# The first stage of a decoder trunk: x loaded and turned by quarters of its channels instead of by halves

## The chip, the core and the metric

The kernel runs on one core of one Trainium2 chip. The core has TensorE (PE, with its weight loads on the separate row PEld), VectorE (DVE), ScalarE (ACT), GpSimd (POOL) and SyncE (SP). SP and ACT each issue transfers on a queue of their own, and all transfers run on the same 16 DMA engines. The metric is the device time of one execution in microseconds (us). In the trace, times are counted from the start of the span.

## The reference, cut to what matters

One decoder layer is computed for a prompt of 512 positions and for 8 samples of 8 positions, 576 rows of 1024 channels in all, with the same weights. In float32:

```python
mod = silu(c) @ w_ada + b_ada               # c: 1 prompt row and 8 sample rows
sh1, sc1, g1, sh2, sc2, g2 = split(mod, 6)
u = x * (1 + sc1) + sh1                     # shared input of both token mixers
z = u @ w_in                                # [pool | q | f | i | out_gate | gate_A | gate_B]
y_pool = pool_mixer(z_pool)                 # 512 channels, causal means over 2, 4, 8, 16 tokens
y_hgrn = hgrn2(z_q, z_f, z_i, z_og, lb)     # lb from softmax(lb_logits)
x = layer_norm(ALPHA * x + g1 * (merged @ w_out))
x = layer_norm(ALPHA * x + g2 * (silu(h @ w_gate) * (h @ w_up)) @ w_down)   # h = x * (1 + sc2) + sh2
```

The change lies wholly in the first stage: from the loads of x, c and the small vectors to z_pool, the first 512 columns of z.

## The kernel before, in words

**Channels on partitions.** u is wanted with its 1024 channels on the partitions, as 8 blocks of 128 channels (kt = 0 to 7) by 576 columns. x comes with its rows on partitions, in tiles of 128 rows by 512 channels (four of the prompt, one of 64 rows of the samples); `x_load` loads one half of the channels (5 tiles), and `x_turn` turns a half on TensorE into PSUM (L304, L309) and copies it to XT on ACT and DVE (L305, L311).

**Scale and shift.** `ada` makes 256 columns of mod: w_ada comes in two tiles of 512 KB, eight products with c go side by side on the array (L339), the four partial rows are copied out (adaev, L343) and summed by another product (L345), and the bias is added (mod, L347). A pair of channel blocks needs one such block of sc1 and one of sh1. ACT then makes uh, the part of u that is rounded for the fast product (L397), and u itself (L402); DVE makes the sample columns (L398 to L401) and ul, the remainder u - uh (L403).

**Products.** Each weight tile is split in the same way: whi on ACT (L111), wlo on DVE (L112). A product is three matmuls: wlo by uh, whi by ul, whi by uh. For z_pool the five row tiles of u are the stationary operand and 512 columns of w_in the moving one; the sums of all 8 channel blocks stay in five PSUM banks (zp, L417). The loop over b = 0 to 3 handles two channel blocks each: it makes u for the pair, runs `ada1(b + 1)` for the next pair, then the pair's 30 products. I call the four pairs quarter 0 to quarter 3. After quarter 3 the weights of z_f follow (L154), and then the rest of the layer.

**What sets the order.** The tile layer schedules the recorded instructions with a timeline of its own, so the order on an engine is not that of the code. Every engine runs its instructions in order. A tile with a number of buffers is reused in turn: the weight tiles raw, whi and wlo have 3 buffers, the w_ada tiles 8, the x tiles 10, and the PSUM tile t, in which x is turned and `ada` sums, has 2. The transfers of SP and ACT take turns on eight completion semaphores; each transfer waits until the one eight places before it has landed.

**Queues.** Before the change SP issues c, the first half of x, w_ada for quarter 0 (with six small vectors, `rows`, between its two blocks: b_ada, lb_logits, norm weights and the like, L285), the first tile of w_in, w_ada for quarter 1, the second half of x, the second tile of w_in, and so on. ACT issues the constants (cst, L98) and a copy of the old pooling state.

Of the kernel before, what the change touches and what calls it, by code (L numbers as in the profile page):

```python
# [12 lines left out]
P = 128  # L13
D = 1024
KT = D // P
TP = 512
# [57 lines left out]
def trunk(tc, consts, x_prompt, x_sample, state_pool, state_hgrn, c_prompt, c_sample,  # L74
# [20 lines left out]
    sp.dma_start(out=cc[0:1], in_=c_prompt)  # L95
    sp.dma_start(out=cc[1:9], in_=c_sample)
    cst = t_(cp, [P, C_END], "cst")
    act.dma_start(out=cst, in_=consts[:, 0:C_END])  # L98
    ident = cst[:, C_ID:C_ID + P]
    rows = t_(s0, [92, P], "rows")  # L100
    R_LB, R_NW, R_PS, R_BA, R_LG, R_LO, R_END = 0, 16, 24, 28, 76, 84, 92
    cst_eps = t_(cp, [P, 2], "eps")
# [159 lines left out]
    def x_load(j):  # L262

        xin = []
        for i in range(5):
            n = P if i < 4 else TS
            xt = t_(sx, [P, 512], "x", bufs=10)
            c = slice(j * 512, (j + 1) * 512)
            sp.dma_start(out=xt[:n], in_=x_prompt[0, i * P:(i + 1) * P, c] if i < 4 else xs_flat[:, c])
            xin.append(xt)  # L270
        return xin

    ada_ready = {}

    def ada_pre(b):
        for m in (SC1, SH1):
            ada_ready[m // 2 + b] = ada_load(s0, m // 2 + b)
        return ada_last[0]

    xin = [x_load(0)]  # L280
    ada_ready[SC1 // 2] = ada_load(s0, SC1 // 2)
    for r, src in ((R_BA, b_ada[0]), (R_LB, lb_logits.rearrange("r c -> (r c)")), (R_NW, hgrn_norm_w[0]),
                   (R_PS, pool_scale[0]), (R_LG, ln1_g[0]), (R_LO, ln1_b[0])):
        v = src.rearrange("(h p) -> h p", p=P)
        sp.dma_start(out=rows[r:r + v.shape[0]], in_=v)  # L285
    ada_ready[SH1 // 2] = ada_load(s0, SH1 // 2)
    w0 = [load_w(seq.pop(0))]
    ada_pre(1)
    xin.append(x_load(1))
    w0.append(load_w(seq.pop(0)))  # L290
    ada_pre(2)
    w0.append(load_w(seq.pop(0)))
    late = ada_pre(3)
# [6 lines left out]
    def x_turn(q):  # L300
        for i in range(4):
            ps = t_(psA, [P, 512], "t", bufs=2)
            for k in range(4):
                pe.transpose(out=ps[:, k * P:(k + 1) * P], in_=xin[q][i][:, k * P:(k + 1) * P], identity=ident)  # L304
            (dve.tensor_copy if i % 2 else act.copy)(out=XT[:, 4 * q:4 * q + 4, i * P:(i + 1) * P],  # L305
                                                     in_=ps.rearrange("p (k n) -> p k n", k=4))
        ps = t_(psA, [P, 512], "t", bufs=2)
        for k in range(4):
            pe.transpose(out=ps[:, k * TS:(k + 1) * TS], in_=xin[q][4][:TS, k * P:(k + 1) * P],  # L309
                         identity=ident[:TS, :TS])  # L310
        act.copy(out=XT[:, 4 * q:4 * q + 4, TP:T], in_=ps[:, :4 * TS].rearrange("p (k n) -> p k n", k=4))  # L311

    x_turn(0)
# [11 lines left out]

    mod = t_(cp, [P, 48, 9], "mod")
# [39 lines left out]

    lbt = t_(cp, [P, 6, 8], "lbt")
    lmax, le0, le1, lb, oml, noml = (lbt[:, i] for i in range(6))
    dve.tensor_tensor(out=lmax, in0=prow[:, 0:8], in1=prow[:, 8:16], op=ALU.max)
    dve.tensor_tensor(out=le0, in0=prow[:, 0:8], in1=lmax, op=ALU.subtract)  # L370
    dve.tensor_tensor(out=le1, in0=prow[:, 8:16], in1=lmax, op=ALU.subtract)
    act.activation(out=lbt[:, 1:3], in_=lbt[:, 1:3], func=AF.Exp)
    dve.tensor_tensor(out=lmax, in0=le0, in1=le1, op=ALU.add)
    dve.reciprocal(out=oml, in_=lmax)
    dve.tensor_tensor(out=lb, in0=le0, in1=oml, op=ALU.mult)
    dve.tensor_tensor(out=oml, in0=le1, in1=oml, op=ALU.mult)
    dve.tensor_scalar(out=noml, in0=oml, scalar1=-1.0, scalar2=None, op0=ALU.mult)

# [10 lines left out]
    for b in range(4):  # L389
        us_ = []  # L390
        for kt in (2 * b, 2 * b + 1):
# [11 lines left out]
            dve.tensor_tensor(out=UL[:, kt], in0=u, in1=UH[:, kt].bitcast(F32), op=ALU.subtract)  # L403
        if b < 3:
            ada1(b + 1)
        if b == 0:
# [899 lines left out]
```

## Time and profile before

| | us |
|---|---|
| median of 3 runs | 1022.06 |
| the runs | 1018.23, 1022.06, 3328.05 |
| the profiled execution | 1022.08 |
| its span | 1020.2 |
| TensorE busy | 972.8 (95%) |
| VectorE busy | 784.0 (77%) |
| ScalarE busy | 489.5 (48%) |

A busy share is an average over the span. The first stage lasts until the first product of z_f starts at 63.88 us; what is said of it is read from the chain of waits, the timeline and the DMA rates of that stretch.

### The profile page before, as it was taken

How to read it: one execution, taken by the hardware profiler on the slowest of the kernel's cores; microseconds unless marked ns; L12 is line 12 of the kernel's file. 1: busy time of each engine (PE TensorE's matmuls, PEld its weight loads, DVE VectorE, ACT ScalarE, POOL GpSimd, SP SyncE). 2: the span in 40 equal slices, each digit the busy share in tenths (PEclk: the TensorE clock that was granted, in tenths of full speed). 3: DMA queues.
4: the chain of work that ended last, by engine and by line, in shares of the span. 5: the costliest groups of instructions: out<-in, count | busy, mean ns of one | idle time of the engine just before them, and what ended most of it. 6: DMA issues, size and time to landing. Idle time of an engine off the chain costs nothing.

```text
span 1020.2 us, 17282 instructions
## 1 busy us (share of the span) xinstructions
PE 972.8 (95%) x6675; PEld 887.6 (87%) x6675; DVE 784.0 (77%) x1337; ACT 489.5 (48%) x889; POOL 355.4 (35%) x263
## 2 busy tenths in 40 slices
PE   6999999999999999998988988999999999999995
PEld 3689899999999998778987778999999999788884
DVE  3662989988998664349797788999999998946548
ACT  3454675577656763334333354544444445533330
POOL 0012777677676855724671102222222220000000
PEclk9999999999999999999999999999999999999998
DMA  8951243323332359952318400233233323432202
GB/s 272 313 143 33 69 114 113 87 83 112 101 107 86 103 168 307 293 175 75 92 52 271 131 1 21 83 105 103 84 91 98 103 84 111 139 120 68 90 32 93
DMA packets 157748, 120.54 MB, mean 118 GB/s; under 512 B 3885, under 2 KB 136585, under 8 KB 157659
## 3 DMA queue, kind: packets, MB, share of 16 engines
q1 hardware_dynamic: 155695, 114.67, 37.3%
q10 hardware_dynamic: 1972, 4.78, 1.4%
q8 instruction: 52, 0.85, 0.3%
q14 instruction: 29, 0.24, 0.1%
HBM read 111.15 MB, written 8.40 MB: 117 GB/s over the span
## 4 chain that ended last, share of the span: by engine, by line
PE 63%; DVE 18%; DMA 6%; ACT 5%; issue 5%; POOL 2%; SPq 0%; DVEq 0%; POOLq 0%; ACTq 0%
PE b L217 24%; PE f L217 10%; PE b L1164 4%; PE b L1163 4%; PE b L1162 4%; DMA ada<-in_w_ada 3%; PE z L154 3%; PE zp L417 3%; ACT whi L172 2%; DVE wlo L173 2%; DVE tmp L560 2%; DVE S L658 1%; PE s L723 1%; DVE qz L587 1%; PE b L1168 1%
## 5 line engine op out<-in xcount | busy, mean ns | idle before, releaser
L172 ACT CAST whi<-st 128x512 fp32r<-128x512 f32 x184 | 108.8, 616 | 57.5 <-PE b L217 13.3
L173 DVE TENSOR_TENSOR wlo<-st,whi 128x512 fp32r<-128x512 f32 x140 | 113.4, 835 | 9.7 <-ACT whi L172 4.4
L217 PE MATMUL f<-uh,whi 128*128 128x288 f32 x352 | 105.9, 301 | 0.0
L217 PE MATMUL f<-ul,whi 128*128 128x288 f32 x352 | 104.9, 298 | 0.0
L217 PE MATMUL f<-uh,wlo 128*128 128x288 f32 x352 | 104.1, 296 | 0.0
L197 POOL TENSOR_TENSOR st<-raw 128x512 f32<-128x512 f32 x36 | 55.0, 1528 | 137.7 <-DVE wlo L173 60.8
L172 ACT CAST whi<-raw 128x1024 fp32r<-128x1024 f32 x46 | 48.3, 1050 | 98.1 <-PE b L217 55.5
L112 DVE TENSOR_TENSOR wlo<-raw,whi 128x1024 fp32r<-128x1024 f32 (+1 forms) x49 | 57.9, 1182 | 29.1 <-ACT whi L111 28.0
L198 POOL TENSOR_TENSOR st<-st,raw 128x512 f32<-128x512 f32 x46 | 64.2, 1396 | 39.7 <-issue 37.7
L111 ACT CAST whi<-raw 128x1024 fp32r<-128x1024 f32 (+1 forms) x49 | 48.0, 979 | 58.0 <-PE z L154 9.8
L1164 PE MATMUL b<-whi,hl 128*128 128x512 f32 (+1 forms) x198 | 72.6, 367 | 0.0
L1163 PE MATMUL b<-whi,hl 128*128 128x512 f32 (+1 forms) x198 | 72.5, 366 | 0.0
L1162 PE MATMUL b<-wlo,hl 128*128 128x512 f32 (+1 forms) x198 | 72.4, 365 | 0.0
L203 POOL TENSOR_TENSOR st<-raw,st 128x512 f32<-128x512 f32 x26 | 42.4, 1632 | 85.9 <-DVE wlo L173 85.9
L173 DVE TENSOR_TENSOR wlo<-raw,whi 128x1024 fp32r<-128x1024 f32 x46 | 57.3, 1246 | 18.9 <-ACT whi L172 18.7
L217 PEld LDWEIGHTS f<-uh,whi 128*128 128x128 f32 x352 | 66.1, 188 | 4.5 <-issue 1.7
L217 PEld LDWEIGHTS f<-ul,whi 128*128 128x128 f32 x352 | 66.1, 188 | 3.5 <-issue 3.4
L217 PEld LDWEIGHTS f<-uh,wlo 128*128 128x128 f32 x352 | 66.1, 188 | 2.8 <-issue 2.5
L173 POOL TENSOR_TENSOR wlo<-st,whi 128x512 fp32r<-128x512 f32 x44 | 58.3, 1333 | 5.7 <-ACT whi L172 5.2
L217 PE MATMUL b<-bh,whi 128*128 128x288 f32 x184 | 55.1, 300 | 2.1 <-ACT bh L172 2.1
L217 PE MATMUL b<-bl,whi 128*128 128x288 f32 x184 | 54.3, 296 | 0.0
L217 PE MATMUL b<-bh,wlo 128*128 128x288 f32 x184 | 54.1, 295 | 0.0
(454 smaller groups left out, 3180.8 us busy)
## 6 DMA issues: line engine op xcount, KB each, us to landing
raw<-in_w_in SPq DMA_DIRECT2D x52, 512.0 KB
ada<-in_w_ada SPq DMA_DIRECT2D x16, 1024.0 KB
raw<-in_w_gate SPq DMA_DIRECT2D x22, 512.0 KB
raw<-in_w_down SPq DMA_DIRECT2D x22, 512.0 KB
ada<-in_w_ada SPq DMA_DIRECT2D x16, 512.0 KB
raw<-in_w_up SPq DMA_DIRECT2D x12, 512.0 KB
rawu<-in_w_up SPq DMA_DIRECT2D x10, 512.0 KB
s<-in_state_hgrn SPq DMA_DIRECT2D x8, 512.0 KB
```

The lines of the kernel that those rows point to most:

```text
L111: act.copy(out=hi[:, :n], in_=raw[:, :n])
L112: eng.tensor_tensor(out=lo[:, :n], in0=raw[:, :n], in1=hi[:, :n].bitcast(F32), op=ALU.subtract)
L154: mm = pe.matmul(out=ps[:, GA0 + c0:GA0 + c1], lhsT=a[:, kt * P:(kt + 1) * P], rhs=x[:, kt, c0:c1], start=first and i == 0, stop=last and ...
L172: act.copy(out=hi, in_=src)
L173: return eng.tensor_tensor(out=lo, in0=src, in1=hi.bitcast(F32), op=ALU.subtract)
L197: pool.tensor_tensor(out=s1, in0=a21, in1=a22, op=ALU.add)
L198: pool.tensor_tensor(out=s2, in0=s1, in1=a11, op=ALU.subtract)
L203: eng.tensor_tensor(out=s4, in0=a12, in1=s2, op=ALU.subtract)
L217: pe.matmul(out=ps, lhsT=x[:, k * P:(k + 1) * P], rhs=y[:, k], start=first and k + i == 0, stop=last and k == 3 and i == 2)
L1162: pe.matmul(out=o, lhsT=xh, rhs=lo, start=first, stop=False)
L1163: pe.matmul(out=o, lhsT=xl, rhs=hi, start=False, stop=False)
L1164: return pe.matmul(out=o, lhsT=xh, rhs=hi, start=False, stop=last)
```

## The change

x comes in four quarters of 256 channels (five tiles of 128 rows by 256 channels each, still ten buffers). `quarter_load` issues for one quarter: x, the two blocks of w_ada, the tile of w_in. Two quarters are issued ahead, the others from inside the loop. c and the six small vectors are issued by ACT, ahead of its first table load. `x_turn(0)` stands behind the turning of c. The lower bound (lbt) is written behind the loop.

```diff
--- before.py
+++ after.py
@@ -92,13 +92,17 @@
     s0, _s0 = pl.open("s0", "right")
     sx, _sx = pl.open("sx", "right")
     cc = t_(s0, [9, D], "cc")
-    sp.dma_start(out=cc[0:1], in_=c_prompt)
-    sp.dma_start(out=cc[1:9], in_=c_sample)
     cst = t_(cp, [P, C_END], "cst")
     act.dma_start(out=cst, in_=consts[:, 0:C_END])
+    act.dma_start(out=cc[0:1], in_=c_prompt)
+    act.dma_start(out=cc[1:9], in_=c_sample)
     ident = cst[:, C_ID:C_ID + P]
     rows = t_(s0, [92, P], "rows")
     R_LB, R_NW, R_PS, R_BA, R_LG, R_LO, R_END = 0, 16, 24, 28, 76, 84, 92
+    for r, src in ((R_BA, b_ada[0]), (R_LB, lb_logits.rearrange("r c -> (r c)")), (R_NW, hgrn_norm_w[0]),
+                   (R_PS, pool_scale[0]), (R_LG, ln1_g[0]), (R_LO, ln1_b[0])):
+        v = src.rearrange("(h p) -> h p", p=P)
+        act.dma_start(out=rows[r:r + v.shape[0]], in_=v)
     cst_eps = t_(cp, [P, 2], "eps")
     dve.memset(cst_eps[:, 0:1], RMS_EPS)
     dve.memset(cst_eps[:, 1:2], LN_EPS)
@@ -264,33 +268,24 @@
         xin = []
         for i in range(5):
             n = P if i < 4 else TS
-            xt = t_(sx, [P, 512], "x", bufs=10)
-            c = slice(j * 512, (j + 1) * 512)
+            xt = t_(sx, [P, 256], "x", bufs=10)
+            c = slice(j * 256, (j + 1) * 256)
             sp.dma_start(out=xt[:n], in_=x_prompt[0, i * P:(i + 1) * P, c] if i < 4 else xs_flat[:, c])
             xin.append(xt)
         return xin
 
-    ada_ready = {}
-
-    def ada_pre(b):
+
+    xin, ada_ready, w0 = [], {}, []
+
+    def quarter_load(b):
+        xin.append(x_load(b))
         for m in (SC1, SH1):
             ada_ready[m // 2 + b] = ada_load(s0, m // 2 + b)
+        w0.append(load_w(seq.pop(0)))
         return ada_last[0]
 
-    xin = [x_load(0)]
-    ada_ready[SC1 // 2] = ada_load(s0, SC1 // 2)
-    for r, src in ((R_BA, b_ada[0]), (R_LB, lb_logits.rearrange("r c -> (r c)")), (R_NW, hgrn_norm_w[0]),
-                   (R_PS, pool_scale[0]), (R_LG, ln1_g[0]), (R_LO, ln1_b[0])):
-        v = src.rearrange("(h p) -> h p", p=P)
-        sp.dma_start(out=rows[r:r + v.shape[0]], in_=v)
-    ada_ready[SH1 // 2] = ada_load(s0, SH1 // 2)
-    w0 = [load_w(seq.pop(0))]
-    ada_pre(1)
-    xin.append(x_load(1))
-    w0.append(load_w(seq.pop(0)))
-    ada_pre(2)
-    w0.append(load_w(seq.pop(0)))
-    late = ada_pre(3)
+    quarter_load(0)
+    quarter_load(1)
 
     psA, _psA = pl.open("psA", space=PSUM)
 
@@ -298,19 +293,20 @@
     XT = t_(s0, [P, KT, T], "xt")
 
     def x_turn(q):
-        for i in range(4):
+        for i in (0, 2):
             ps = t_(psA, [P, 512], "t", bufs=2)
-            for k in range(4):
-                pe.transpose(out=ps[:, k * P:(k + 1) * P], in_=xin[q][i][:, k * P:(k + 1) * P], identity=ident)
-            (dve.tensor_copy if i % 2 else act.copy)(out=XT[:, 4 * q:4 * q + 4, i * P:(i + 1) * P],
-                                                     in_=ps.rearrange("p (k n) -> p k n", k=4))
+            for j in range(2):
+                for k in range(2):
+                    pe.transpose(out=ps[:, k * 256 + j * P:k * 256 + (j + 1) * P],
+                                 in_=xin[q][i + j][:, k * P:(k + 1) * P], identity=ident)
+            (dve.tensor_copy if i else act.copy)(out=XT[:, 2 * q:2 * q + 2, i * P:(i + 2) * P],
+                                                 in_=ps.rearrange("p (k n) -> p k n", k=2))
         ps = t_(psA, [P, 512], "t", bufs=2)
-        for k in range(4):
+        for k in range(2):
             pe.transpose(out=ps[:, k * TS:(k + 1) * TS], in_=xin[q][4][:TS, k * P:(k + 1) * P],
                          identity=ident[:TS, :TS])
-        act.copy(out=XT[:, 4 * q:4 * q + 4, TP:T], in_=ps[:, :4 * TS].rearrange("p (k n) -> p k n", k=4))
-
-    x_turn(0)
+        act.copy(out=XT[:, 2 * q:2 * q + 2, TP:T], in_=ps[:, :2 * TS].rearrange("p (k n) -> p k n", k=2))
+
 
     sc_ = t_(s0, [9, D], "sc")
     act.activation(out=sc_, in_=cc, func=AF.Sigmoid)
@@ -323,6 +319,7 @@
     dve.tensor_copy(out=cpad[:, :, 0:9],
                     in_=pc[:, :P].rearrange("p (k c) -> p k c", c=16)[:, :, 0:9])
 
+    x_turn(0)
     mod = t_(cp, [P, 48, 9], "mod")
 
     dr, _dr = pl.open("gada", space=bass.MemoryType.DRAM)
@@ -363,19 +360,6 @@
 
     ps0 = [t_(psA, [P, 512], "zp", bufs=5) for i in range(5)]
     ada1(0)
-
-    lbt = t_(cp, [P, 6, 8], "lbt")
-    lmax, le0, le1, lb, oml, noml = (lbt[:, i] for i in range(6))
-    dve.tensor_tensor(out=lmax, in0=prow[:, 0:8], in1=prow[:, 8:16], op=ALU.max)
-    dve.tensor_tensor(out=le0, in0=prow[:, 0:8], in1=lmax, op=ALU.subtract)
-    dve.tensor_tensor(out=le1, in0=prow[:, 8:16], in1=lmax, op=ALU.subtract)
-    act.activation(out=lbt[:, 1:3], in_=lbt[:, 1:3], func=AF.Exp)
-    dve.tensor_tensor(out=lmax, in0=le0, in1=le1, op=ALU.add)
-    dve.reciprocal(out=oml, in_=lmax)
-    dve.tensor_tensor(out=lb, in0=le0, in1=oml, op=ALU.mult)
-    dve.tensor_tensor(out=oml, in0=le1, in1=oml, op=ALU.mult)
-    dve.tensor_scalar(out=noml, in0=oml, scalar1=-1.0, scalar2=None, op0=ALU.mult)
-
     YA = t_(ym, [P, 4, T], "ya")
     YB = t_(ym, [P, NH, T], "yb")
 
@@ -401,11 +385,14 @@
             dve.tensor_copy(out=UH[:, kt, TP:T], in_=u[:, TP:T])
             act.activation(out=u[:, 0:TP], in_=XT[:, kt, 0:TP], func=AF.Identity, scale=sc[:, 0:1], bias=sh[:, 0:1])
             dve.tensor_tensor(out=UL[:, kt], in0=u, in1=UH[:, kt].bitcast(F32), op=ALU.subtract)
+        if b < 2:
+            late = quarter_load(b + 2)
         if b < 3:
+            x_turn(b + 1)
             ada1(b + 1)
+        if b == 2:
+            pl.close(_sx)
         if b == 0:
-            x_turn(1)
-            pl.close(_sx)
             tu, _tu = pl.open("tu", "left")
             TU = t_tiles(tu, ("t1", "t2", "t4"))
         for kt in (2 * b, 2 * b + 1):
@@ -425,9 +412,19 @@
                 dve.tensor_tensor(out=tc_[:, k], in0=u[:, HT:T], in1=tc_[:, k], op=ALU.subtract)
         for n, t, k0, k1 in ((), (("t1", ta, 0, 4),), (("t2", tb, 0, 2),), ())[b]:
             split(*(x[:, k0:k1] for x in TU[n]), t[:, k0:k1])
-        if b == 0:
-            w0.append(load_w(seq.pop(0)))
     pl.close(_s0)
+
+    lbt = t_(cp, [P, 6, 8], "lbt")
+    lmax, le0, le1, lb, oml, noml = (lbt[:, i] for i in range(6))
+    dve.tensor_tensor(out=lmax, in0=prow[:, 0:8], in1=prow[:, 8:16], op=ALU.max)
+    dve.tensor_tensor(out=le0, in0=prow[:, 0:8], in1=lmax, op=ALU.subtract)
+    dve.tensor_tensor(out=le1, in0=prow[:, 8:16], in1=lmax, op=ALU.subtract)
+    act.activation(out=lbt[:, 1:3], in_=lbt[:, 1:3], func=AF.Exp)
+    dve.tensor_tensor(out=lmax, in0=le0, in1=le1, op=ALU.add)
+    dve.reciprocal(out=oml, in_=lmax)
+    dve.tensor_tensor(out=lb, in0=le0, in1=oml, op=ALU.mult)
+    dve.tensor_tensor(out=oml, in0=le1, in1=oml, op=ALU.mult)
+    dve.tensor_scalar(out=noml, in0=oml, scalar1=-1.0, scalar2=None, op0=ALU.mult)
 
     def zt():
         return t_(psZ, [P, D], "z", bufs=2)
```

On all five engines the instructions from the first product of z_f on stand in the same order as before; what moves lies ahead of it. Three places.

ACT, between the u of quarter 0 and that of quarter 1 (whi is the rounded weight tile, raw the loaded one, uh the rounded u, xt the turned x). Before:

```order
L402 ACTIVATE yb_266<-xt_165,mod_211 128x512
L111 CAST whi_136<-raw_134 128x1024
L305 COPY xt_165<-t_307 128x4x128
L397 ACTIVATE uh_84<-xt_165,mod_211 128x512
L402 ACTIVATE yb_266<-xt_165,mod_211 128x512
L397 ACTIVATE uh_84<-xt_165,mod_211 128x512
```

Now:

```order
L386 ACTIVATE yb_220<-xt_143,mod_175 128x512
L302 COPY xt_143<-t_257 128x2x256
L115 CAST whi_136<-raw_134 128x1024
L308 COPY xt_143<-t_269 128x2x64
L115 CAST whi_253<-raw_251 128x1024
L115 CAST whi_374<-raw_372 128x1024
L381 ACTIVATE uh_90<-xt_143,mod_175 128x512
```

The casts of the third and fourth weight tiles (raw_251, raw_372) now stand ahead of quarter 1's uh; before, they stood behind it. On DVE the remainder of the fourth tile now stands ahead of quarter 1's ul:

```order
L116 TENSOR_TENSOR wlo_375<-raw_372,whi_374 128x1024
L385 CAST uh_90<-yb_220 128x64 x2
L302 COPY xt_143<-t_384 128x2x256
L407 TENSOR_TENSOR yb_220<-yb_220 128x288
L387 TENSOR_TENSOR ul_91<-yb_220,uh_90 128x576 x2
```

ACT, ahead of quarter 0, now (t is the PSUM tile with two buffers, in which x_turn and `ada` take turns):

```order
L302 COPY xt_143<-t_159 128x2x256
L115 CAST whi_112<-raw_110 128x1024
L308 COPY xt_143<-t_171 128x2x64
L422 ACT_TABLE_LOAD
L422 ACTIVATE lbt_604<-lbt_604 128x16
L381 ACTIVATE uh_90<-xt_143,mod_175 128x512
```

The copy of the turned sample tile out of t_171 stands behind the cast of the first weight tile, and the first product of `ada` (t_191) takes t_171's buffer. The exponential of the lower bound still stands ahead of quarter 0's u.

SP, the third round of loads, now:

```order
L273 DMA x_241<-in_x_sample 64x256
L261 DMA ada_243<-in_w_ada 128x4x256
L261 DMA ada_245<-in_w_ada 128x4x256
L129 DMA raw_251<-in_w_in 128x2x512
L261 DMA ada_247<-in_w_ada 128x4x256
L129 DMA raw_372<-in_w_in 128x2x512
L261 DMA ada_249<-in_w_ada 128x4x256
```

The fourth weight tile, raw_372, is loaded behind three quarters of x, eleven tiles of w_ada and three of w_in.

## Rows read from the trace of the kernel before

**Rows 1.** Chain of waits, 0 to 110 us: start us, us, what

```profile
23.82 2.43 PE zp L417 x5
...
37.03 0.44 PE t L304 x4
37.47 3.66 PE zp L417 x16
41.13 0.39 PE t L309 x4
41.52 1.00 PE t L339 x16
...
63.88 6.39 PE z L154 x48
```

**Rows 2.** Timeline, ACT's first casts, one product: start, us, engine, operation, [idle before, releaser]

```profile
18.07 1.08 PE L339 MATMUL t<-ada,cpad 128*32 128x256 f32 x8 [0.53 <-DMA ada<-in_w_ada]
...
19.70 1.04 ACT L111 CAST whi<-raw 128x1024 fp32r<-128x1024 f32 x1 [3.72 <-DMA raw<-in_w_in]
...
30.83 1.05 ACT L111 CAST whi<-raw 128x1024 fp32r<-128x1024 f32 x1 [5.71 <-DMA raw<-in_w_in]
```

**Rows 3.** DMA issues by line, 0 to 80 us: tile, source, count, KB each

```profile
ada<-in_w_ada SPq DMA_DIRECT2D x16, 512.0 KB
raw<-in_w_in SPq DMA_DIRECT2D x11, 512.0 KB
x<-in_x_prompt SPq DMA_DIRECT2D x8, 256.0 KB
...
cst<-in_consts ACTq DMA_DIRECT2D x1, 263.0 KB
```

**Rows 4.** DMA totals of three windows: 0 to 18, 0 to 31, 0 to 36 us

```profile
DMA packets 3357, 4.23 MB, mean 235 GB/s; under 512 B 244, under 2 KB 2416, under 8 KB 3349
...
DMA packets 7029, 8.71 MB, mean 281 GB/s; under 512 B 425, under 2 KB 5219, under 8 KB 7020
...
DMA packets 8655, 10.47 MB, mean 291 GB/s; under 512 B 475, under 2 KB 6698, under 8 KB 8646
```

**Rows 5.** Busy time by stretch; the last three columns: granted clock, DMA share, GB/s

```profile
12.00:13.00 1.00, 0.91 (x8) 0.81 (x8) 0.00 (x0) 0.98 (x2) 0.00 (x0) 1.00 0.39 86
...
30.00:36.00 6.00, 5.81 (x37) 4.66 (x34) 2.86 (x8) 2.56 (x4) 0.00 (x0) 1.00 1.09 353
```

**Rows 6.** Timeline, SP's queue: first of the six small vectors, next w_ada tile

```profile
7.00 0.33 SPq L285 DMA_DIRECT2D rows<-in_b_ada  x1
...
11.64 1.93 SPq L257 DMA_DIRECT2D ada<-in_w_ada  x2
```

**Rows 7.** Groups by shape, 0 to 64 us: busy us, mean ns of one, idle before

```profile
L112 DVE TENSOR_TENSOR wlo<-raw,whi 128x1024 fp32r<-128x1024 f32 x6 | 7.3, 1220 | 1.5 <-ACT whi L111 1.3
...
L397 ACT ACTIVATE uh<-xt,mod 128x512 fp32r<-128x512 f32 x8 | 6.5, 807 | 9.9 <-DVE mod L347 9.9
...
L403 DVE TENSOR_TENSOR ul<-yb,uh 128x576 fp32r<-128x576 f32 x4 | 3.0, 751 | 0.4 <-ACT yb L402 0.4
L305 DVE COPY xt<-t 128x512 f32<-128x512 f32 x4 | 2.8, 689 | 4.1 <-PE t L304 4.1
...
L420 DVE TENSOR_TENSOR yb<-yb 128x288 f32<-128x288 f32 x4 | 1.8, 450 | 0.0
...
L401 DVE CAST uh<-yb 128x64 fp32r<-128x64 f32 x4 | 0.6, 188 | 0.0
```

**Rows 8.** Timeline, TensorE after two idle times: start, us, operation, [idle before]

```profile
524.70 0.58 PE L217 MATMUL f<-t3h,whi 128*128 128x288 f32 x1 [2.05 <-DVE u L230]
...
539.61 0.38 PE L217 MATMUL f<-t3h,whi 128*128 128x288 f32 x1 [1.98 <-DVE u L230]
```

**Rows 9.** Busy time by stretch, behind each of those two

```profile
524.70:528.00 3.30, 3.30 (x14) 3.30 (x15) 3.30 (x4) 1.77 (x3) 2.22 (x2) 0.50 0.11 40
...
536.00:543.00 7.00, 5.02 (x38) 4.82 (x37) 6.76 (x12) 4.29 (x5) 0.24 (x1) 1.00 0.46 165
```

## The prediction

> **What bounds the kernel now.** I read the chain of waits first. In the first stage it runs from the first product at 23.82 us almost without a break along TensorE to 63.88 us, where z_f starts [rows 1]; ahead of 23.82 it runs along transfers. The timeline gives the two places where ACT sat before a weight cast and waited for the transfer: 3.72 us until 19.70 for the first tile, 5.71 us until 30.83 for the second [rows 2]. The list of DMA issues gives the sizes [rows 3], the DMA totals how much had moved by then [rows 4], and the busy time by stretch the rates, 86 GB/s at 12 to 13 us and 353 GB/s later [rows 5]. So the stage is transfers up to 23.8 us, then TensorE, fed by transfers with some us to spare. The instructions behind 63.88 us stand in the old order, so I take a shift of that point as the shift of the end. The profiled execution took 1022.08 us, the median is 1022.06, so either may be the base.
>
> **When a tile lands.** Count KB in the order of issue. Up to the first weight tile stood half of x (four tiles of 256 KB and one of 128), four w_ada tiles, the weights themselves, the constants [rows 3], and about 194 KB of small transfers: 4169 KB, 4.27 MB. It was there at 19.70, when the DMA had moved 4.23 MB by 18 us [rows 4] and 1.7 us at 353 GB/s [rows 5] more, 4.83 in all. The second tile: 7881 KB, 8.07 MB, there at 30.83, with 8.71 MB moved by 31 us, so 8.65 at that time. In both cases a tile was there when 0.56 to 0.58 MB more had moved than stood up to it. I use 0.58.
>
> **The change part by part.**
>
> *Smaller head.* Up to the first weight tile now stand 576 KB less of x: 3593 KB, 3.68 MB, so 4.26 MB must have moved. On the old curve that is 18.1 us.
>
> *Small vectors to ACT's queue.* SP had w_ada waiting behind six small transfers, from 7.00 to 11.64 us [rows 6], and the DMA fell to 86 GB/s for the microsecond from 12 [rows 5]. At 353 GB/s that gap is 0.8 us; I take it as gained, with bounds of 0 (the gap stays) and 1.5 us (some of the slow stretch around it goes as well). The first tile is then there at 17.3 instead of 19.7 us. [...]
>
> *ACT's longer start.* Eight issues at about SP's 0.33 us each [rows 6], some with a wait, stand ahead of the table load and the sigmoid of c. That puts c's turning at 10 to 11 us. Products with c need the first w_ada tiles anyway, and, see next, something later: cost nothing; without this cover 2 us.
>
> *Quarter 0.* The first product of `ada` takes the PSUM buffer of the turned sample tile, whose copy stands on ACT behind the first weight cast. So it starts at 17.3 + 1.05 + about 0.5 = 18.9 us instead of before the weights. Before, from a group of eight such products at 18.07 [rows 2] to the first z product took 5.75 us; now the other block's 16 records come on top, 2.2 us at 1.08 per eight. First z product at 26.8 us, later than the old 23.82, at most; it is 2 to 3 us earlier if TensorE is at its full clock by then, at which 16 such records take 1.00 us [rows 1]. Quarter 0 has 30 products at 3.66 / 16 = 0.23 us, 6.9 us, and 32 records of quarter 1's `ada`, 2.0 us: done at 35.7 us.
>
> *Quarter 1 behind the fourth weight tile.* On ACT the casts of the third and fourth tile now stand ahead of quarter 1's uh. The fourth tile reuses the buffers of the first, so its cast waits for quarter 0's last product (35.7 us) and for its own transfer. Up to that transfer stand three quarters of x (1728 KB), eleven w_ada tiles, four weight tiles, constants and small ones: 9865 KB, 10.10 MB, so 10.68 MB must have moved. The old curve has 10.47 MB at 36 us [rows 4], so 36.6, less the 0.8 of the gap: 35.8 us. Both conditions come together. Then follow the cast 1.05 [rows 2], and on DVE wlo 1.22, two sample casts 0.38, the copy of turned x 0.69, one difference 0.45, ul 0.75 [rows 7]: 4.5 us. Quarter 1's products with ul start at 40.3 us; before, at 37.47 [rows 1]. That is 2.9 us late (40.3 - 37.47, rounded up for the hand-overs). Bounds: with transfers at 353 GB/s from 2.2 us on, the tile would land at 32.5 us and only quarter 0 would decide, up to 3 us earlier than taken: 0. With the gap kept and a further microsecond lost to the ten more issues: 4.7.
>
> *Behind it.* Quarters 1 to 3 have the same products and `ada` records. New there are eight turned tiles, 0.88 us at 0.44 per four, and two small ones, 0.2, where before four small ones took 0.39 [rows 1]: 0.7 us more. Quarter 2's and 3's data land some us ahead of use, since TensorE then needs about 10 us for a quarter (6.9 + 2.0 + 0.9, and the sums of `ada`) and the transfers (576 + 2048 + 512 KB) 9.1 us.
>
> *Nothing else.* Ten more x issues on SP lie beside its waits for landings; two more small copies out of PSUM lie beside products; the lower bound's nine small operations stay where they were, ahead of quarter 0's u on DVE and ACT, so nothing is taken off the path. Without this cover each is below 0.5 us.
>
> Sum: 2.9 + 0.7 = 3.6 us, 1022.1 + 3.6 = **1025.7 us**; with the bounds of its terms 1022.8 to 1028.
>
> **Rivals.**
>
> *The quarters do bring the stage forward.* The first weight tile comes 2.4 us earlier; if the fourth tile has landed by 30 us and TensorE is up to speed early, quarter 1 isn't held and the 2.4 us stay: 1019.7. For it: 576 KB less stand ahead of everything. Against it: even at 353 GB/s without a gap the fourth tile takes until 32.5 us.
>
> [...]
>
> *The gap stays*, because the eight places for outstanding transfers now fill with small x tiles: everything 0.8 us later, 1026.5.
>
> *The change does nothing here*, since the last half of the stage is TensorE's and loads were ahead of it: 1022.1. For it: the unbroken chain from 37 to 64 us.
>
> **Numbers.** Chances: forecast 0.50, quarters forward 0.18, clock drop 0.14, gap stays 0.10, nothing 0.08. The likeliest case alone spans 1022.8 to 1028; the range takes in the faster rival and the clock drop, 1018.5 to 1030, with some 1.5 us of scatter at the ends; about 0.15 is left out. 2% is 20 us, about what a measurement of this kernel can tell from no change. [...] Faster by over 2%: 0.01, within 2%: 0.97, slower: 0.02.
>
> **What would show it.** ACT waiting for a transfer ahead of the fourth weight cast, at about 34 to 37 us, and TensorE idle or waiting for uh and ul behind quarter 0; the first weight cast at 17 to 18 us, the first z product at 24 to 27 us; z_f starting at 67 to 68 us instead of 63.88; everything behind shifted alike. I am wrong if the fourth tile is cast before 33 us, if quarter 1's products follow quarter 0's without a gap, or if the shift at z_f doesn't reach the end.

## The result and the profile after

| | kernel before | changed kernel |
|---|---|---|
| median of seven runs, us | 1022.06 (1018.23 to 1023.52, and one of 3328) | 1027.20 (1025.36 to 1029.54) |
| ratio, 95% interval | 1 | 1.006 (1.0041 to 1.008) |
| profiled execution, its span | 1022.08, 1020.2 | 1026.67, 1024.6 |
| first product of z_f | 63.72 | 69.29 |

The ratio leaves the run of 3328 us out; the six others of the kernel before have a median of 1021.29. In a second series (e7) the changed kernel had 1026.34 us against 1021.99, ratio 1.0047 (1.0031 to 1.0064). So it is slower by about half a percent, 4.4 to 5.9 us by the medians; the forecast was 1025.7, +3.6.

The chain of waits of the changed kernel (start, us, what) answers to [rows 1]. The lines of code have moved: L417 is L404, L304 is L300, L339 is L336, L345 is L342, L154 is L158.

```profile
26.88 8.63 DMA raw<-in_w_in
35.60 0.63 ACT whi L115
36.23 0.32 issue
36.55 0.82 ACT uh L381
37.42 2.04 PE zp L404 x5
39.46 0.40 PE t L306 x2
39.86 4.39 PE zp L404 x15
...
53.21 1.93 PE t L336 x32
...
69.45 6.39 PE z L158 x48
```

Where the old chain ran along TensorE from 23.82 us on, the new one still comes from a transfer at 35.60: the fourth weight tile, its cast, quarter 1's uh. The timeline of ACT's casts answers to [rows 2] (start, us, engine, operation, [idle before, releaser]):

```profile
15.73 1.04 ACT L115 CAST whi<-raw 128x1024 fp32r<-128x1024 f32 x1 [2.89 <-DMA raw<-in_w_in]
...
25.81 1.06 ACT L115 CAST whi<-raw 128x1024 fp32r<-128x1024 f32 x1 [0.26 <-DMA raw<-in_w_in]
...
32.66 1.04 ACT L115 CAST whi<-raw 128x1024 fp32r<-128x1024 f32 x1 [5.64 <-DMA raw<-in_w_in]
35.60 1.05 ACT L115 CAST whi<-raw 128x1024 fp32r<-128x1024 f32 x1 [1.89 <-DMA raw<-in_w_in]
36.55 0.81 ACT L381 ACTIVATE uh<-xt,mod 128x512 fp32r<-128x512 f32 x1
```

The tiles land earlier than before (15.73 for 19.70, 25.81 for 30.83). But ACT waits for the third and the fourth with quarter 1's uh behind them. VectorE does the same with the third tile's remainder, and TensorE waits for both (timelines of DVE and PE):

```profile
33.74 1.23 DVE L116 TENSOR_TENSOR wlo<-raw,whi 128x1024 fp32r<-128x1024 f32 x1 [3.91 <-ACT whi L115]
34.89 0.42 DVE L340 COPY adaev<-t 128x256 f32<-128x256 f32 x1
```

```profile
35.36 0.61 PE L342 MATMUL t<-cst,adaev 128*128 128x9 f32 x4 [2.31 <-DVE adaev L340]
35.83 1.07 PE L300 MATMUL t<-cst,x 128*128 128x128 f32 x8
37.42 2.04 PE L404 MATMUL zp<-wlo,uh 128*128 128x512 f32 x5 [0.52 <-ACT uh L381]
```

The eviction adaev at 34.89 could have been done some us earlier: its product had run at 28.3 to 30.2 us. It stands on VectorE behind a remainder whose tile was still in flight. The busy time by stretch (the length, the busy time and instructions of PE, PEld, DVE, ACT and POOL, then granted clock, DMA share, GB/s) and the DMA total to 36 us answer to [rows 4, 5]:

```profile
12.00:13.00 1.00, 1.00 (x6) 0.67 (x4) 0.00 (x0) 0.59 (x1) 0.00 (x0) 1.00 1.06 366
30.00:36.00 6.00, 3.69 (x24) 2.93 (x21) 2.01 (x5) 1.44 (x2) 0.00 (x0) 1.00 1.08 361
...
38.00:41.40 3.40, 3.40 (x10) 2.13 (x9) 2.78 (x7) 2.74 (x6) 0.00 (x0) 0.50 1.09 347
```

```profile
DMA packets 10165, 11.05 MB, mean 307 GB/s; under 512 B 632, under 2 KB 8995, under 8 KB 10156
```

The gap at 12 us is gone (366 GB/s for 86), 11.05 MB have moved by 36 us for 10.47, TensorE is busy 3.69 of 6 us for 5.81, and behind its wait it ran 3.4 us at a granted clock of 0.50. The transfers gained; the order of what waits for them lost.

**How I add up the stage.** The loss lies ahead of z_f: in 13 of the 14 profiles of this study the run is 954 to 959 us longer than the start of z_f (963 in e3), 958.4 in the kernel before and 957.2 to 957.4 in the changed one. The first ul product of quarter 1 and the first product of z_f, before and now:

```profile
37.54 0.39 PE L417 MATMUL zp<-whi,ul 128*128 128x512 f32 x1
...
63.72 0.42 PE L154 MATMUL z<-uh,whi 128*128 128x256 f32 x2
```

```profile
39.80 0.80 PE L404 MATMUL zp<-whi,ul 128*128 128x512 f32 x1
...
69.29 0.42 PE L158 MATMUL z<-uh,whi 128*128 128x256 f32 x2
```

Two stretches each of the kernel before and of the changed one, split at the first z product (columns as above):

```profile
0.00:23.75 23.75, 13.96 (x85) 7.88 (x85) 7.73 (x28) 8.19 (x12) 0.52 (x5) 1.00 0.87 264
23.75:63.72 39.97, 39.78 (x248) 29.00 (x245) 28.28 (x66) 20.02 (x28) 1.04 (x2) 1.00 0.82 249
```

```profile
0.00:23.02 23.02, 9.46 (x67) 6.43 (x68) 7.15 (x28) 6.59 (x10) 0.52 (x5) 1.00 0.88 282
23.02:69.29 46.27, 42.05 (x263) 29.52 (x263) 28.66 (x67) 21.65 (x32) 1.05 (x2) 0.96 0.70 210
```

TensorE's idle time ahead of z_f is 9.99 us before (23.75 - 13.96 + 0.19) and 17.79 after: 3.77 us more ahead of the first z product, 4.03 more behind it. From the time at the low clock, granted 0.50, half is lost. Ahead of its first change the column of the granted clock reads 1.00, so I read the level there from durations: eight turnings take 1.95 us where the column reads 0.50 (e1, 50.12 us) and 1.07 where it reads 1.00 behind the rise (changed kernel, 35.83 us); the 1.97 us at 11.11 us in the changed kernel I then read as the low level. I take the idle time and half of the low-clock busy time off z_f; what is left is the work, counted at the full clock (my readings are good to about 0.5 us):

| profile | z_f | idle | busy at the low clock | left: work |
|---|---|---|---|---|
| before | 63.7 | 10.0 | 16.4 | 45.5 |
| changed kernel | 69.3 | 17.8 | 11.3 | 45.9 |
| changed kernel again (e7) | 68.8 | 16.4 | 13.0 | 45.9 |
| e1, third and fourth tile's split later | 73.5 | 19.2 | 16.9 | 45.9 |
| e5, third to sixth | 67.1 | 14.8 | 11.2 | 46.7 |
| e6, c and the rows on SP's queue | 68.0 | 11.2 | 17.3 | 48.2 |
| e9, x turned ahead of c | 68.2 | 13.0 | 17.4 | 46.5 |
| e10, e9 and ties and a third PSUM buffer | 64.9 | 11.2 | 13.8 | 46.9 |
| e11, e10 and c's sigmoid first | 61.3 | 11.4 | 8.2 | 45.7 |

But for e6 the work differs by 1.4 us at most; the kernels differ mostly in idle time, and the executions in the clock. In e6 the 96 scale and shift products of quarters 1 to 3 stand in nine groups among the others and take 7.2 us, counted from the start of a group to the start of what follows, less waits; in e5 they stand in three groups and take 5.6.

### The profile page after: what moved, and what is told of

It is laid out like the page before. It is cut to its first block, busy times and chain, and to the rows that moved or that the text cites. A ratio compares the mean times of both kernels' runs of the same rounds, so it can differ in the third digit from the quotient of the medians.

```text
span 1024.6 us, 17305 instructions
## 1 busy us (share of the span) xinstructions
PE 970.6 (95%) x6675; PEld 886.9 (87%) x6675; DVE 781.5 (76%) x1337; ACT 489.6 (48%) x891; POOL 355.2 (35%) x263
## 4 chain that ended last, share of the span: by engine, by line
PE 69%; DVE 14%; DMA 6%; issue 4%; ACT 4%; POOL 2%; SPq 0%; DVEq 0%; POOLq 0%; ACTq 0%
PE b L221 24%; PE f L221 15%; PE b L1161 4%; PE b L1160 4%; PE b L1159 4%; PE z L158 3%; PE zp L404 2%; DMA raw<-in_w_in 2%; PE s L720 1%; DVE S L655 1%; DVE tmp L557 1%; ACT whi L176 1%; DMA ada<-in_w_ada 1%; DVE wlo L177 1%; PE s L679 1%
```

## The experiments

Theory: the splits of late weight tiles stand in the engines' order ahead of work that is ready, and that holds TensorE (order theory). Rivals: the quarters' smaller transfers are late themselves (transfer theory); the low clock carries most of the loss (clock theory). Each run's times stand beside the kernel before on the same chip (one chip for e1 to e4, one for e5 to e8, one for e9 and e10, one for e11 and e12). A tie, `issue_after` in the code, makes the scheduler place an instruction behind a named one.

**e1: the third and fourth tile's splits behind quarter 1's u.** The split is taken out of the load and issued behind the last u on ACT and the last ul on DVE.

```diff
+    def late_split(q, a, d):
+        with contextlib.ExitStack() as c:
+            c.enter_context(tc.issue_after(a.ins))
+            c.enter_context(tc.issue_after(d.ins))
+            split_w(*w0[q])
+        w0[q] = w0[q][1:]
...
+                    late_split(q, u_act, u_dve)
```

> The changed kernel, but the splits of the third and fourth weight tile (cast on ScalarE, remainder on VectorE) stand behind quarter 1's u on both engines. Order theory (the splits in front of quarter 1's u hold TensorE until those tiles land): TensorE's idle 2.31 us at 33 to 35.4 us and the half clock at 38 to 41.4 us go, quarter 1's ul products start at 34 to 36 us (39.80 in the changed kernel), z_f at 63.5 to 65.5 us (69.45), the time falls to 1021.5 to 1023.5 us, that is 0 to +2 us against the kernel before. Transfer theory (the quarters' smaller transfers make x or the scale and shift weights late): the idle stays at the same place with another releaser, z_f at 68 us or later, 1026 to 1028 us. Clock theory (most of the loss is the low clock, which any idle there brings on): if an idle of 1 us or more stays, the clock falls all the same and the gain is under 2 us.

Measured: 1030.68 us, ratio 1.009 (1.0063 to 1.0118); z_f 73.54. Half of what was expected came: TensorE had no idle time from 22.7 to 44.4 us, quarter 1's ul products started at 36.01 us (39.80). Then the same wait, one tile later (PE, and DVE around it):

```profile
49.25 1.02 PE L352 MATMUL t<-cst,adaev 128*128 128x9 f32 x4 [4.83 <-DVE adaev L350]
```

```profile
47.63 1.23 DVE L116 TENSOR_TENSOR wlo<-raw,whi 128x1024 fp32r<-128x1024 f32 x1 [4.13 <-ACT whi L115]
48.77 0.42 DVE L350 COPY adaev<-t 128x256 f32<-128x256 f32 x1
```

The scheduler had put the fifth tile's remainder ahead of quarter 2's eviction, and behind the 4.83 us of idle time TensorE ran at a granted clock of 0.50 until about 54.9 us. One more wait, 1.21 us ahead of 64.79 for uh behind the sixth tile's cast, was followed by the low level too (five products in 2.26 us, 1.32 at 57.10). The expected time was wrong by 7 us; the mechanism was seen twice.

**e2: the fourth tile's split alone** (the same edit with `LATE = (3,)`).

> As the run before, but only the fourth tile's split is moved behind quarter 1's u; the third stays in front. If the third tile holds TensorE (its remainder stands on VectorE ahead of the eviction that the shift of quarter 1 needs): the idle of 2.31 us stays, ul products from 38 to 39 us, z_f 67.5 to 68.5 us, 1025 to 1026.5 us. If the fourth tile holds it, as the prediction said: ul products at 36.5 to 37.5 us, z_f 65 to 66 us, 1022.5 to 1024 us.

Measured: 1032.55 us, 1.0105 (1.0077 to 1.0132); z_f 73.79. The idle time stayed, 2.63 us until 36.02, and the ul products started at 39.96 us: moving the fourth tile alone won nothing at quarter 1. The third tile, which I had not counted, holds TensorE just as long. (Later an eviction behind the fifth tile's remainder cost 1.23 us, and uh behind the sixth tile's cast 1.21.) The place of the wait was as expected, the time was missed by 6 us. The third tile's split alone was not moved in any run, so what the fourth costs by itself is not shown.

**e3: TensorE kept busy in its idle time.**

```diff
+        pf = t_(psA, [P, 512], "fill", bufs=1)
+        with tc.issue_after(a.ins):             # between the two sums of quarter 1's scale and shift
+            for i in range(10):
+                a = pe.matmul(out=pf, lhsT=UH[:, 0, 0:P], rhs=half(w0[1][0], 0), start=True, stop=True)
```

In the same edit the second sum is tied behind the ten products, and quarter 3's loads behind quarter 1's sample columns.

> The changed kernel with ten more products of 512 columns on TensorE (into a PSUM tile that nothing reads) in the idle time at 32.9 to 35.4 us, so that the engine is busy there; the order on every engine is otherwise the same. It prices the clock alone. Order theory: the clock stays full at 38 to 41.4 us, but the ul products wait for VectorE's remainders until 39.8 us anyway, so only the half clock behind 39.8 us is won: z_f 0.8 to 1.2 us earlier (68.2 to 68.7 us), 1026 to 1026.6 us. Clock theory: most of the +5 us is the clock, z_f at 66 to 67.5 us, 1023.5 to 1025.5 us. If the clock falls all the same, no change (1027 us).

Measured: 1031.04 us, 1.009 (1.0065 to 1.0115); z_f 71.08. No case that was written down came, and the run settles nothing: in its profile the clock rose at about 28 us instead of 21, quarter 0's products ended at 35.5 instead of 32.7, and the ten products (2.56 us) then stood in the way instead of in idle time. The clock did stay at 1.00 at 38 to 41 us, but that priced nothing.

**e4: one part of the change alone, in the kernel before: c and the small rows issued by ACT.**

```diff
-    sp.dma_start(out=cc[0:1], in_=c_prompt)
+    act.dma_start(out=cc[0:1], in_=c_prompt)
...
-        sp.dma_start(out=rows[r:r + v.shape[0]], in_=v)
+        act.dma_start(out=rows[r:r + v.shape[0]], in_=v)      # moved ahead of the table load
```

> The kernel before with one part of the change alone: c and the small rows are issued by ScalarE's queue. The order that follows from it puts the third weight tile's split ahead of quarter 1's u, and ScalarE's sample tile copy behind nothing new. Order theory: transfers 0.5 to 1 us earlier, but quarter 1's u waits for the third tile, which lands at about 35 to 36 us: z_f 64 to 66 us (63.88 in the kernel before), +0.5 to +2 us against the kernel before. If the small rows on the other queue are what costs: +4 us or more. If quarters of x carry the whole loss: -1 to 0 us.

Measured: 1020.80 us, 1.0002 (0.9988 to 1.0016); z_f 62.88. This part costs nothing and brings the tiles forward: 17.18 for 19.70, and then (ACT)

```profile
29.25 1.05 ACT L115 CAST whi<-raw 128x1024 fp32r<-128x1024 f32 x1 [4.03 <-DMA raw<-in_w_in]
30.62 1.05 ACT L115 CAST whi<-raw 128x1024 fp32r<-128x1024 f32 x1 [0.32 <-DMA raw<-in_w_in]
31.67 0.82 ACT L397 ACTIVATE uh<-xt,mod 128x512 fp32r<-128x512 f32 x1
```

Here too the third tile's cast stands ahead of quarter 1's uh, as in the changed kernel; but it had landed, so ACT waited 0.32 us. So the place in the order did harm where the tile landed late, and not here. The expected +0.5 to +2 us did not come, since the third tile had landed by 30.6 us and not at 35 to 36. The lower bound's move was not run by itself; in the changed kernel its operations still stand ahead of quarter 0's u, at 18.4 to 20.3 us on VectorE.

**e5: the fifth and the sixth tile's splits too**, behind quarter 2's and quarter 3's u.

```diff
-    with tc.issue_after(late.ins):
+    with tc.issue_after(late.ins), tc.issue_after(u_act_[2].ins), tc.issue_after(u_dve_[2].ins):
+        prefetch(1)
+    with tc.issue_after(late.ins), tc.issue_after(u_act_[3].ins), tc.issue_after(u_dve_[3].ins):
         w = next_w()
```

> The run with the third and fourth tile's splits moved showed the wait again one tile later (TensorE idle 4.83 us at 44.4 us, for a scale and shift eviction that VectorE does behind the fifth tile's remainder, whose tile landed at 46.5 us). Here the fifth tile's split too stands behind quarter 2's u, and the sixth behind quarter 3's; the loads keep their order. Order theory: no idle over 1 us on TensorE between 23 and 64 us, z_f at 62.5 to 65 us (69.29 in the changed kernel), 1019.5 to 1022.5 us, within 1.5 us of the kernel before. Transfer theory: an idle of 2 us or more stays, released by x, by a scale and shift weight or by the landing of a tile; 1025 us or more. Clock theory (the low clock is chance and not caused by the idle): z_f early, but the clock falls in 30 to 60 us all the same and 1 to 2 us of the gain are lost: 1022 to 1025 us.

Measured: 1024.26 us, 1.0024 (1.0008 to 1.004); z_f 67.11. Between 23.5 and 57.5 us no idle time is left, with the quarters' transfers as they are; that speaks against the transfer theory. About half of the loss is back: 2.1 us by the medians against the changed kernel in this series (1.0047), though the two intervals overlap. The expected 1019.5 to 1022.5 us was missed by 2 us. What is left: 13.9 us of idle time ahead of the first z product, as in the changed kernel, and one wait, with no split ahead of it on VectorE, with the low clock behind it:

```profile
58.32 2.21 PE L422 MATMUL zp<-wlo,uh 128*64 128x512 f32 x5 [0.77 <-DVE uh L396]
```

```profile
58.32:62.00 3.68, 3.68 (x9) 2.58 (x10) 2.66 (x7) 3.41 (x5) 1.04 (x2) 0.60 0.00 0
```

**e6: the changed kernel with c and the rows back on SP's queue** (e4's edit the other way round).

> The changed kernel with one part undone: c and the small rows are issued by SyncE's queue again, the rows between the two scale and shift blocks of quarter 0. In the order that comes of it the third and fourth tile's splits stand behind quarter 1's u and quarter 1's and 2's evictions ahead of the next tile's remainder. Order theory: the quarters of x themselves cost nothing: no idle over 1 us on TensorE between 23 and 64 us, z_f at 63 to 66 us, 1019.5 to 1023 us. If the quarters are what costs (smaller transfers, the weight tiles between them): 1026 us or more, whatever the order. If the rows on SyncE's queue cost at the start: first z product 0.5 to 1.5 us later than in the changed kernel (23.0 us).

Measured: 1026.19 us, 1.0043 (1.0025 to 1.006); z_f 68.00. The order is as wanted, the idle time is 11.18 us and the first z product comes at 20.82; but from quarter 2's turning of x to quarter 3's TensorE takes 12.5 us (32.64 to 45.16), where e5 takes 11.8 (33.87 to 45.69), and behind waits of 0.77, 0.34 and 0.30 us at 58 to 61 us the low clock came again (0.57 over 60 to 64 us). Against e5 the idle time is 3.6 us less, the low clock takes 3 us more and the work 1.5 us more, for the shorter groups named above. So a right place for the splits is not enough; my expectation missed by 3 us.

**e7: the changed kernel again.**

> The changed kernel as it is, beside the others on the same chip: 1025.4 to 1029.6 us, +4 to +8 us against the kernel before. Its profile is a second look at the waits and at the moment at which TensorE's clock rises, which was 20.9 us in its first profile and about 26.3 us in that of the kernel before: the order theory expects the idle time at 33 to 35.4 us in the same place (2 to 2.7 us) and z_f at 69 to 72 us, by the moment of the rise.

Measured: 1026.34 us, 1.0047 (1.0031 to 1.0064); z_f 68.78. The clock rose at about 26.4 us, quarter 0 ended 2 us later, and the wait shrank:

```profile
35.76 0.61 PE L342 MATMUL t<-cst,adaev 128*128 128x9 f32 x4 [0.58 <-DVE adaev L340]
...
40.04 0.50 PE L404 MATMUL zp<-whi,ul 128*128 128x512 f32 x1 [0.70 <-DVE ul L387]
```

No drop of the clock followed, TensorE spent less time at the low clock than in the kernel before (13.0 us for 16.4), and z_f came only 0.5 us earlier than in the first profile. So quarter 1 is held by the landing, whatever TensorE did before, and the drop in the first profile was no main cause: the clock theory falls.

**e8: e6, and eight products on zeros ahead of everything.**

```diff
+    for i in range(8):
+        pe.matmul(out=pf[:, 0:256], lhsT=cpad[:, 0:4], rhs=cpad, start=True, stop=True)
```

> As the run with the rows on SyncE's queue, and TensorE runs eight products of 128 by 256 (float32, zeros, into PSUM that nothing reads) before its first transposes, about 4 us of work from 1.5 us on. It asks whether the moment of the clock's rise (20.6 to 28.2 us in the profiles so far) is moved by earlier work. If it is: the scale and shift products of quarter 0 (3.64 us for 32 at the low clock) take 1.9 us, quarter 0's products are at full clock, 1 to 3 us less than without, and the spread of the runs shrinks. If the gap behind the eight products lets the clock fall again, or earlier work does not count: no difference.

Measured: 1025.98 us, 1.004 (1.0022 to 1.0057), against 1.0043 for e6: no difference. The clock did rise early, and fell again (first eight turnings; then a stretch):

```profile
8.06 1.12 PE L306 MATMUL t<-cst,x 128*128 128x128 f32 x8
```

```profile
13.69:27.00 13.31, 11.16 (x56) 6.25 (x57) 6.87 (x21) 4.60 (x7) 0.00 (x0) 0.50 1.01 334
```

**e9: one line of the change undone, x turned ahead of c.**

```diff
+    x_turn(0)
     sc_ = t_(s0, [9, D], "sc")
...
-    x_turn(0)
     mod = t_(cp, [P, 48, 9], "mod")
```

> The changed kernel with one line of it undone: the turning of x's quarter 0 is written ahead of c's sigmoid and turning again, as in the kernel before. In the order that comes of it TensorE turns x first, ScalarE copies the sample tile ahead of the first weight tile's cast, and (with no word about it in the program) the third and fourth tile's splits stand behind quarter 1's u on both engines. In the profiles so far the time is the start of z_f plus 956.0 to 958.4 us in ten of eleven, and TensorE's idle time ahead of z_f is 9.99 us in the kernel before, 17.79 and 16.43 us in the changed one. Order theory: x is turned from 7 to 9 us on (11.11 in the changed kernel), the scale and shift products start at 12 to 14.5 us (17.04), idle ahead of z_f falls to 10 to 12.5 us, z_f at 62.5 to 65.5 us, 1020 to 1023.5 us. Transfer theory (the quarters' loads themselves hold TensorE): idle stays at 15 us or more and 1025 us or more. If only the start is won and the tiles hold quarter 1 all the same: first z product at 20 to 21 us, but z_f at 67 us or later, 1025 us or more.

Measured: 1025.20 us, 1.0051 (1.003 to 1.0072); z_f 68.16. With this line alone the scheduler puts the third and fourth tile's splits behind quarter 1's u, and TensorE has no idle time from 22.5 to 58.2 us; the scale and shift products start at 12.14 us (17.04). But two further splits take over (PE):

```profile
18.97 2.07 PE L343 MATMUL t<-cst,adaev 128*128 128x9 f32 x8 [3.33 <-DVE adaev L341]
...
59.39 2.24 PE L405 MATMUL zp<-wlo,uh 128*128 128x512 f32 x5 [1.21 <-ACT uh L382]
```

At 18.97 an eviction stood behind the first tile's remainder (its tile landed at 15.81), at 59.39 uh behind the sixth tile's cast, which waited for a buffer. Idle time 12.95 us, near the forecast; but 17.4 us ran at the low clock, so z_f missed by 3.

**e10: e9, the ties of e1 and e5, and three PSUM buffers for t instead of two.**

> The run before this one, with the splits of the third to sixth tile also tied behind quarter 1's, 2's and 3's u, and three PSUM buffers instead of two for what is turned and for the scale and shift products (the changed kernel's product that waited 0.8 us at 53.2 us for a copy of x out of such a buffer, and the first scale and shift product, have one more). Order theory: the least idle of all, 8 to 11 us ahead of z_f, z_f at 61 to 64 us, 1018.5 to 1021.5 us: as the kernel before or up to 2 us under it. If the third buffer counts for nothing: as the run before this one, within 1 us. If the longer rows of products of one kind that the other order breaks up cost TensorE more: z_f at 65 us or later although the idle is below 11 us.

Measured: 1019.46 us, 0.9988 (0.9971 to 1.0006); z_f 64.93 in its profile, 0.22 us of idle time from 24.35 us to z_f. This is level with the kernel before, and its interval lies below both of the changed kernel's. In its profile turnings and scale and shift products run among the products of the quarter before, and u is ready when the quarter starts. What is due to the third buffer and what to the ties was not separated, and the kernel before was not run with a third buffer; so the level time does not show that the quarters by themselves cost nothing.

**e11 and e12: the start.** e11 issues the rows on ACT behind c's sigmoid; e12 also puts the first tile's remainder behind quarter 0's evictions, the second's behind the first's.

```diff
+    sg_ = act.activation(out=sc_, in_=cc, func=AF.Sigmoid)
+    with tc.issue_after(sg_.ins):
+        ...                                                   # the six rows' loads
+    with tc.issue_after(md0.ins):                              # e12: behind quarter 0's mod
+        lo0 = split_w(*w0[0], part=2)
```

> The run with all splits tied and three PSUM buffers (median 1019.46 us), and on ScalarE's queue the issues of the six small row transfers stand behind c's sigmoid instead of ahead of its table load. In the kernel before the sigmoid of c starts at 4.06 us, in the changed kernel at 7.82, behind nine issues from 0.74 to 6.39 us and the table load. If these issues hold the start: sigmoid at 4 to 4.6 us (8.80 in the run with the splits tied), c's turning at 7 to 8 us on TensorE (11.24), the scale and shift products at 10.5 to 12.2 us (12.67) by the landing of their weights; but the eviction that they need stands behind the first tile's remainder on VectorE (18.68 us), so the first z product moves by 0 to 1 us from 24.35 and the time by 0 to 1 us: 1018.5 to 1019.5 us. If the landing of the scale and shift weights decides the start: no difference.

> The other run of this call, and the first tile's remainder stands on VectorE behind quarter 0's scale and shift evictions, the second tile's remainder behind the first's. Order theory: the eviction at 13.5 to 15.5 us (18.68), first z product at 18.5 to 21 us (24.35), idle ahead of z_f 8 to 11 us, z_f at 61.5 to 64 us (64.93), 1016 to 1018.8 us: under the kernel before by 3 to 6 us. If the landing of quarter 1's scale and shift weights and of quarter 2's x, whose products now stand among quarter 0's, takes the place of the wait: idle of 2 us or more at 20 to 27 us, and 1018.5 to 1020 us.

Measured: e11 1019.87 us, 0.9992 (0.9974 to 1.0011), z_f 61.25; e12 1021.59 us, 1.0001 (0.9982 to 1.002), z_f 62.78. Neither is faster than e10. The profile of e11 is that of the fastest of its twelve executions (1015.37 us), so its early z_f is not typical of it. The sigmoid started at 5.50 us and c was turned at 8.82 (11.24 in e10), as the theory of the start asked; but the rows, issued later, then landed later, and their turning stands ahead of the scale and shift products on TensorE (e11):

```profile
8.82 0.99 PE L332 MATMUL t<-cst,sc 9*128 9x9 f32 x8 [1.12 <-DVE sc L110]
14.70 0.39 PE L362 MATMUL t<-cst,rows 92*128 92x92 f32 x1 [4.89 <-DMA rows<-in_ln_b]
15.02 3.64 PE L349 MATMUL t<-ada,cpad 128*32 128x256 f32 x32
```

Wait for wait: 4.89 us for the rows where e10 had 3.70 for c. I had named the landing of the weights as the rival, not that of the rows. In e12 the eviction came no earlier than 18.65, since its products started at 14.79.

## Why the prediction came out right

The forecast, +3.6 us through a late tile at quarter 1, was the case that came. Its steps:

*Landing.* First tile forecast 17.3, measured 15.73; fourth 35.8, measured 35.60, with ACT waiting for it and uh behind it, as said. The gap at 12 us was gained. That both came so near is in part luck: I let a tile be there when 0.58 MB more had moved than stood up to it, and it was 0.45 MB for the first (4.13 MB by 15.7 us) and 0.78 for the fourth (10.88 MB by 35.5 us); against that, more had moved than the 0.8 us of the gap account for (11.05 MB by 36 us for 10.47, 1.6 us at 361 GB/s). e4 shows the earlier first tiles by itself: with the rows alone on ACT's queue the first tile came 2.5 us and the second 1.6 us earlier; in the kernel before, SP's queue stood 4.64 us on the six rows [rows 6].

*ACT's longer start.* c turned at 10 to 11: measured 10.16. That the first scale and shift product would wait for the sample tile's copy behind the first cast: right, at 17.04 (forecast 18.9); with the copy ahead it started at 12.14 (e9). "Cost nothing" can't be called shown: the start has 3.77 us more idle time than before, but quarter 1 waits for a landing, so how much of that reaches z_f stays open.

*Quarter 0.* First z product 23.02 (forecast up to 26.8), done at 32.7 (35.7), since the clock rose early; in e7 it was done at 34.8. As quarter 1 waits for a landing, nothing followed from it.

*Quarter 1.* ul products at 39.80 and 40.04 us, forecast 40.3; late by 2.3 and 2.5 us against 37.54 in the kernel before (the 37.47 of the sum is where a piece of the chain begins), forecast 2.9. The cause was half right. I gave it to the fourth tile on ACT; e2 shows that the third tile's remainder on VectorE, ahead of an eviction, holds TensorE as long. I had followed ACT's order there and not VectorE's.

*Behind it* is the step that failed: forecast 0.7 us, measured 3.3 (69.29 - 63.72 - 2.26, with 2.26 = 39.80 - 37.54), and 2.6 in e7, where the clock didn't fall (68.78 - 63.72 - 2.50). In e7 1.36 us of it are three waits of 0.25, 0.83 and 0.28 us at 50 to 63 us (uh behind the fifth tile's cast, a copy of x out of one of two PSUM buffers, a ul), which the sum had at nothing; the other 1.2 are busy time (27.38 us for 26.18), of which the turned tiles, forecast at 0.7, take 1.0 (1.43 us for 0.39). In the first profile the low clock adds 0.8. "Quarter 2's and 3's data land some us ahead of use" was right and not enough: what they stand behind on their engines counts. e5 took the first two of these waits away, e10 all but 0.22 us.

*The end.* I let a shift of z_f reach the end whole. It was 5.6 and 5.1 us at z_f and 4.6 and 3.9 in the profiled executions; behind z_f 1.0 to 1.2 us came back. Why was not followed; it is less than the 5 us by which that rest differs between the profiles, so it is not shown to be an effect of the change. This error and the one above have opposite signs, so it is partly luck that the forecast was off by only 1.5 us (2.3 when the six runs are the base).

*Rivals.* The range up to 1030 counts a clock drop. Behind one of two idle times of about 2 us the granted clock was 0.50, behind the other 1.00 [rows 8, 9], and no run had shown what a drop costs in this stage. Measured, it came in one of two profiles (0.50 at 38.0 to 41.4 us) and cost about 0.8 us at z_f, because ul wasn't ready before 39.80 anyway and only 1.60 us behind it ran at half the clock; z_f was 0.5 us later than in the profile without it. "Quarters forward" was ruled out by the landing of the third and fourth tile; e10 shows the quarters level with the kernel before, with a third buffer beside them, not that they gain. "The gap stays" is refuted by 366 GB/s.

## What to carry to other kernels

Splitting a load to get its first part sooner also changes what a scheduler with its own timeline puts ahead of what: look on every engine, not only on the one with the transfer, for an instruction that waits for a late tile with ready work behind it. Tying such instructions behind that work must go on until the wait has no next tile to move to (e1, then e5, then e10, which had a third buffer too); moving only one tile or two left it slower than the changed kernel (1.0105 and 1.009 for 1.0047 to 1.006, with intervals that still touch). And where the engine that bounds a stage has constant work (here 45.5 to 46.9 us in eight of nine profiles), idle time plus half of its time at a granted clock of 0.50 accounts for the stage, and shows at once whether a change moved a wait or removed it; e6 shows that the work has to be looked at too, since the same products in shorter groups took 1.6 us more.

## What was not expected of the hardware

The moment at which TensorE's clock rises differs between executions far more than the kernels do: read from durations it was about 20.9 us (e1), 21.2 and 26.4 (the same changed kernel twice) and 28 (e3), after the same products from about 17 us on. Half of those seven us is 3.5, as large as the effect that was forecast. In the kernel before, half of the 16.4 us at the low clock is 8.2 us, 0.8% of the span.

Short idle times were followed by the low level in some profiles (0.77 us in e5, granted 0.60 over the 3.68 us behind it; 1.21 in e9, five products in 2.24 us behind it, 1.32 at 51.36) and not in others (0.80 at 55 us in e12, 1.00 over 53 to 58; 0.58, 0.36 and 0.70 in a row in e7, 1.00 over 34 to 42). e6 and e8 have the same three waits of 0.77, 0.34 and 0.30 us ahead of quarter 3's first products; the granted clock was then 0.57 over 60 to 64 us in e6 and 1.00 over 60 to 70 in e8. From one profile a drop can't be priced into a forecast.
